# The down projection of a hybrid encoder block: another order of its seven products

## The chip, the cores and the metric

The kernel runs on one NeuronCore of one Trainium2 chip. The metric is the device time of one execution in microseconds (us), lower is better; the times shown are medians over executions on the chip.

## The reference

One layer of an encoder for 512 tokens of width 2048, all in float32. Cut to what matters here:

```python
D_MODEL, SEQ, D_FF = 2048, 512, 5632

def reference(x, g_mix, w_in, ..., w_out, g_ffn, w_gate_up, w_down, g_final):
    h = rmsnorm(x, g_mix[layer])
    proj = jnp.einsum('bsd,de->bse', h, w_in[layer])
    ...                                   # two kinds of attention over the parts of proj
    x = x + jnp.einsum('bse,ed->bsd', mixed, w_out[layer])
    h2 = rmsnorm(x, g_ffn[layer])
    gate, up = jnp.split(jnp.einsum('bsd,df->bsf', h2, w_gate_up[layer]), 2, axis=-1)
    x = x + jnp.einsum('bsf,fd->bsd', jax.nn.silu(gate) * up, w_down[layer])
    return rmsnorm(x, g_final)
```

The change is in the product with `w_down` (5632 x 2048).

## The kernel before, in words

**Products in fp32 from three.** A float32 operand is split into a high and a low half of the reduced type fp32r. `mm3` then issues three matmuls (lines 242, 243, 244): high by high, high by low, low by high.

**Seven products for eight.** The big projections go by 2x2 blocks in a form with seven products, m1 to m7, where a plain one has eight. Each product needs a left operand (a "form" of the activations, computed once, parked in DRAM as `forms`) and a right one of the weights. In the down stage m1, m2 and m3 use a weight tile as it was loaded; m7, m6, m5 and m4 use a sum or difference of two tiles, which VectorE (DVE) computes at line 872 in `weights`.

**Blocks and units of the down stage.** The inner dimension is cut into groups of 6, 8 and 8 pairs of row tiles (`DOWN_PAIRS`), and each group is done for two halves of the columns, so there are six blocks, which the text counts from 0 to 5. In a block each of the seven products has 6 or 8 *units*, one for a pair: a block has 42 or 56 units. A unit is one entry of the list `units`; its product is six matmuls on TensorE (PE), two row tiles by three. Before them stand, for a unit with a sum, the sum on DVE (line 872); then for every unit the high half of the weights on ScalarE (ACT, line 828) and the low half on DVE (line 831). The halves go into one of eight `tw` pairs, so the high half of unit u waits for the matmuls of unit u - 8.

**What sets the order.** One Python loop goes through the units. `prepare` issues the high halves as long as they are planned within `COLS_AHEAD` = 8.0 us of the present unit (a unit counts 1.37) and the low half of all but the last of these; `load_raws` issues the weight loads (tiles `raw`, on SyncE's queue) as far as `COLS_LOAD` = 20.0 us ahead. Then come the unit's matmuls, then what was hooked to its number with `box.after`. Each engine executes its instructions in the order in which they were issued, ACT's DMA issues among its activations.

**Banks.** A product's units accumulate in PSUM. m1, m6, m5 and m3 share the pair of banks called z, m7 and m4 have y, m2 has x. After the last unit of a product ACT evicts the pair (tiles `ev`, line 1216, two instructions) and GpSimd adds it to the result in DRAM. The sums in a shared bank go on: m6 accumulates onto m1 after the eviction of m1, m5 onto m6 after that of m6. So the first unit of m6 and of m5 waits for that eviction.

**Forms of the next group.** Forms that are done with give place to those of the next group. `next_forms` hooks, for each form and each four pairs: a load on ACT's queue into one of two tiles `fr` (line 1190), the high half on ACT (line 1193) and the low half on DVE (line 1196), 128 x 1024 each. They spread from the end of one group into the first block of the next.

**The order of the products** in the blocks but the last, for n pairs, is: all m1, all m7, all m6, two of m2, all m5, the rest of m2, all m4, all m3. The names here: `raw_N` weight tiles, `tw_N` pairs of halves, `arenaN` the forms in place, `fr_N` forms as loaded, `ev_N` evicted rows, `bN` PSUM banks.

Of the kernel before, what the change touches and what calls it, by code (L numbers as in the profile page):

```python
# [64 lines left out]
def f32(ap):  # L65
    return ap.bitcast(F32)
# [3 lines left out]
def encoder_block(ctx, tc, x, g_mix, w_in, g_q_a, g_k_a, g_out_a, g_out_b, w_out, g_ffn,  # L70
# [80 lines left out]
    def form_tile(m, pairs):  # L151
        return arena[0][:, m, pairs] if m < EARLY else arena[1][:, m - EARLY, pairs]
# [99 lines left out]
    def in_turn(tiles, n, shape, dtype, tag):  # L252
        if not tiles and homing[0]:
            whole = sp.tile([P, n] + shape[1:], dtype, tag=tag + "s", bufs=1, name=nm(tag))
            tiles.extend(whole[:, i] for i in range(n))
        if not tiles:
            tiles.extend(sp.tile(shape, dtype, tag=tag, bufs=n, name=nm(tag)) for _ in range(n))
        tiles.append(tiles.pop(0))
        return tiles[-1]

    class Raw:
        def __init__(self, pieces, first=0, tag="raw", width=2 * 512):
            self.pieces, self.first, self.tag, self.width, self.t = pieces, first, tag, width, None
# [46 lines left out]
    def hook(n, f):  # L310
        hooks.setdefault(n, []).append(f)
# [486 lines left out]
    def drain_until(cond):  # L798
        while not cond():
            side.popleft()()  # L800

    CHAIN = ("m1", "m7", "m6", "m2", "m5", "m4", "m3")
# [4 lines left out]
    KEPT = {"m1": (("a",), "a"), "m7": (("c", "b"), "b"), "m6": (("b", "a"), "b"), "m2": (("d",), "d"),  # L807
            "m5": (("c", "b"), "a"), "m4": (("d", "b"), "b"), "m3": (("c",), "c")}


    class Cols(Unit):
# [21 lines left out]
        def mm(self, u):  # L833
            self.box.multiply(self)

    class ColBlock:
        def __init__(self, w, row, lo, pairs, plan, tag, ready=None, close=None, chain=CHAIN, apart=False):
            self.pairs, self.plan, self.ready, self.close = pairs, plan, ready, close
            self.banks = dict(CHAIN_BANK, m3="x") if apart else CHAIN_BANK
            self.last_of_bank = LAST_OF_BANK + ("m5",) if apart else LAST_OF_BANK  # L840
            self.opening = ("m1", "m7", "m2") + (("m3",) if apart else ())
            self.ps, self.at, self.held = {}, {}, []

            def raw(i, j, q):
                at = row + (2 * q + i) * P
                pieces = lo[j] if isinstance(lo[j], list) else [(lo[j], 0, 512)]
                return Raw(lambda t: [(w[0, at:at + P, c:c + n], t[:, dst:dst + n]) for c, dst, n in pieces],
                           tag=tag, width=512)
            kinds = {"a": (0, 0), "b": (0, 1), "c": (1, 1), "d": (1, 0), "e": (0, 1), "f": (1, 0), "g": (1, 1)}
            self.raws = [{n: raw(i, j, q) for n, (i, j) in kinds.items()} for q in range(pairs)]  # L850
            order = [(form, q) for form in chain for q in range(pairs)]
            if ready is not None:
                rest = order[6:8] + order[8:3 * pairs] + order[3 * pairs + 6:]
                order = order[:6] + order[3 * pairs:3 * pairs + 6] + rest
            if plan is KEPT:
                at = 3 * pairs + 2
                behind = 2 if close is not None else 1
                order[at:at + (1 + behind) * pairs - 2] = (order[at + pairs - 2:at + (1 + behind) * pairs - 2]
                                                           + order[at:at + pairs - 2])
            for form, q in order:  # L860
                self.at[form] = len(units)
                src, dst = plan[form]
                need = src + (dst,) if dst not in src else src
                units.append(Cols(self, form, q, [self.raws[q][n] for n in need]))
                if close is not None and form == CHAIN[-1]:
                    units[-1].dur = COLS_US / 2
# [305 lines left out]
    for f in range(0, NFF, 4):  # L1172
        box = gate_up_block(f)
# [4 lines left out]
            nc.gpsimd.dma_start(x1[c, t], x1_dram[c, t])  # L1178

    def next_forms(box, first, pairs):  # L1180
        seq = sorted(CHAIN, key=box.at.get)

        def ready(form, h):
            m, st = ORDER.index(form), {}
            lo_q, n = 4 * h, min(4, pairs - 4 * h)
            hi, lo = (form_tile(m, slice(lo_q, lo_q + n))[:, :, j] for j in range(2))

            def load():
                st["t"] = in_turn(frs, 2, [P, 4, 256], F32, "fr")[:, :n]
                nc.scalar.dma_start(st["t"], forms_dram[:, m, first + lo_q:first + lo_q + n])  # L1190

            def split_hi():
                nc.scalar.activation(hi, st["t"], AF.Copy)

            def split_lo():
                nc.vector.tensor_tensor(lo, st["t"], f32(hi), op=OP.subtract)  # L1196
            late = 4 * seq.index(form) + 4 * h
            box.after(form, late - 5, load)
            box.after(form, late + 1, split_hi)
            box.after(form, late + 3, split_lo)  # L1200
        for form in seq:
            for h in range(-(-pairs // 4)):
                ready(form, h)
# [121 lines left out]
    for n in DOWN_PAIRS:  # L1325
        next_forms(box, first, n)
        for cb in range(2):
            box = down_block(first, n, cb, (first + n, cb) == (NFF // 2, 1))
        first += n

    at = [0.0]
# [142 lines left out]
```

## Time and profile before

| | |
|---|---|
| time, median of 3 runs | 1985.04 us (1984.05 to 1986.88) |
| the profiled execution | 1985.48 us, of which the span of the trace is 1983.7 us |
| PE busy | 1968.0 us, 99% of the span |
| DVE busy | 1589.3 us, 80% |
| ACT busy | 1131.0 us, 57% |
| mean granted clock of PE | 0.998 |

The down stage runs from about 1549 us to 1970 us of the span. Busy times of PE are modelled from pipelined matmuls, so a PE that is always busy still shows where it loses time: by the distance between the starts of its matmuls, and by the granted clock (1.00 is full speed).

### The profile page before, as it was taken

Reading aid. Unit: us, or ns where it says so; the run is one execution under the profiler, and the core shown is the slowest. Engines: PE = TensorE matmul, PEld = TensorE weight load, DVE = VectorE, ACT = ScalarE, POOL = GpSimd, SP = SyncE. Lnnn points to the kernel's source line nnn. Section 1 sums busy time; section 2 is a strip of 40 time slices with the busy share of each in tenths; the row PEclk is TensorE's granted clock in tenths of the full one; section 3 lists DMA queues with packets and bytes.
Section 4 is the critical chain, followed back from the end, with each engine's and each line's share of the span. In section 5 each row is a group of like instructions: output and inputs, shape, how many; then the busy total and the mean of one; then the engine's idle time right before and its main releaser. Section 6 shows DMA issues by size and latency. Waiting matters only on the chain.

```text
span 1983.7 us, 27526 instructions
## 1 busy us (share of the span) xinstructions
PE 1968.0 (99%) x8972; PEld 1623.0 (82%) x8972; DVE 1589.3 (80%) x2725; ACT 1131.0 (57%) x2071; POOL 120.4 (6%) x162
## 2 busy tenths in 40 slices
PE   9999999999999999999999999999999999999998
PEld 7888887888888888888888888888888888788886
DVE  6888678888775698887878878878879987887977
ACT  7655555565555565555555555545556666666655
POOL 0100001000000000000000000000000121111121
PEclk9999999999999999999999999999999999999999
DMA  8576683143343564755836737657458699769765
GB/s 278 181 281 206 214 276 125 66 144 128 117 151 105 196 206 164 278 167 188 298 124 242 258 128 267 216 174 278 159 192 285 189 276 251 196 158 268 198 162 173
DMA packets 235873, 394.83 MB, mean 199 GB/s; under 512 B 22560, under 2 KB 77648, under 8 KB 235600
## 3 DMA queue, kind: packets, MB, share of 16 engines
q1 hardware_dynamic: 211440, 330.85, 49.6%
q0 software_dynamic: 17200, 40.38, 9.3%
q10 hardware_dynamic: 7088, 21.83, 3.2%
q8 instruction: 70, 1.15, 0.2%
q14 instruction: 75, 0.61, 0.1%
HBM read 330.33 MB, written 62.65 MB: 198 GB/s over the span
## 4 chain that ended last, share of the span: by engine, by line
PE 94%; DVE 3%; ACT 1%; DMA 1%; issue 1%; ACTq 0%; POOL 0%; POOLq 0%; DVEq 0%; SPq 0%
PE b L242 30%; PE b L244 30%; PE b L243 30%; PE b L600 1%; PE b L1145 1%; DMA raw<-in_w_in_dram 1%; DVE raw L872 0%; DVE tw L831 0%; PE b L1069 0%; PE b L326 0%; PE b L550 0%; DVE arena L1196 0%; DVE w L300 0%; ACT rj L435 0%; DVE ra L448 0%
## 5 line engine op out<-in xcount | busy, mean ns | idle before, releaser
L242 PE MATMUL b<-tw,arena 128*128 128x512 f32 x2244 | 880.0, 392 | 2.2 <-ACT ev L1216 2.2
L243 PE MATMUL b<-tw,arena 128*128 128x512 f32 x2244 | 874.6, 390 | 0.3 <-DVE tw L300 0.3
L244 PE MATMUL b<-tw,arena 128*128 128x512 f32 x2244 | 874.6, 390 | 0.0
L828 ACT ACTIVATE tw<-raw 128x512 fp32r<-128x512 f32 x924 | 558.3, 628 | 434.3 <-DVE raw L872 271.6
L831 DVE TENSOR_TENSOR tw<-raw,tw 128x512 fp32r<-128x512 f32 x924 | 618.8, 687 | 167.6 <-ACT tw L828 164.6
L242 PEld LDWEIGHTS b<-tw,arena 128*128 128x128 f32 x2244 | 421.8, 188 | 88.6 <-ACT ev L1216 2.9
L243 PEld LDWEIGHTS b<-tw,arena 128*128 128x128 f32 x2244 | 422.0, 188 | 88.1 <-DVE tw L831 1.4
L244 PEld LDWEIGHTS b<-tw,arena 128*128 128x128 f32 x2244 | 421.7, 188 | 88.2
L872 DVE TENSOR_TENSOR raw<-raw,raw 128x512 f32<-128x512 f32 x528 | 361.1, 685 | 1.4 <-DMA raw<-in_w_gate_up_dram 1.4
L1217 POOL DMA_DIRECT2D x1d<-ev x76 | 66.4, 981 | 1149.3 <-ACT ev L1216 1144.2
L828 ACT ACTIVATE tw<-stage 128x512 fp32r<-128x512 f32 x140 | 85.4, 629 | 67.7 <-DVE stage L872 46.5
L831 DVE TENSOR_TENSOR tw<-stage,tw 128x512 fp32r<-128x512 f32 x140 | 93.6, 687 | 23.5 <-ACT tw L828 23.4
L242 PE MATMUL b<-w,arena 128*128 128x512 f32 x240 | 95.8, 399 | 0.0
L233 ACT ACTIVATE pTh<-b 128x512 fp32r<-128x512 f32 x64 | 38.3, 598 | 100.3 <-PE b L600 96.4
L244 PE MATMUL b<-w,arena 128*128 128x512 f32 x240 | 93.9, 391 | 0.0
L243 PE MATMUL b<-w,arena 128*128 128x512 f32 x240 | 93.5, 390 | 0.0
L365 DVE TENSOR_TENSOR pair<-pair 128x256 f32<-128x256 f32 x120 | 45.5, 421 | 25.0 <-ACT pair L1072 23.9
L1216 ACT ACTIVATE ev<-b,smalls 128x512 f32<-128x512 f32 x76 | 49.6, 682 | 26.3 <-PE b L244 25.3
L1120 DVE TENSOR_TENSOR s<-b,s 128x512 f32<-128x512 f32 x66 | 44.0, 688 | 24.7 <-PE b L244 24.7
L244 PEld LDWEIGHTS b<-w,arena 128*128 128x128 f32 x240 | 45.0, 188 | 10.0
L243 PEld LDWEIGHTS b<-w,arena 128*128 128x128 f32 x240 | 45.2, 188 | 9.1
L242 PEld LDWEIGHTS b<-w,arena 128*128 128x128 f32 x240 | 45.1, 188 | 8.8
(210 smaller groups left out, 1778.9 us busy)
## 6 DMA issues: line engine op xcount, KB each, us to landing
raw<-in_w_gate_up_dram SPq DMA_DIRECT2D x616, 256.0 KB, 5.3
raw<-in_w_down_dram SPq DMA_DIRECT2D x176, 256.0 KB, 6.9
stage<-in_w_in_dram SPq DMA_DIRECT2D x111, 256.0 KB, 5.0
forms<-pair SPq DMA_DIRECT2D x22, 896.0 KB, 5.3
x1d<-ev POOLq DMA_DIRECT2D x76, 256.0 KB, 6.5
fr<-forms ACTq DMA_DIRECT2D x35, 512.0 KB, 6.0
raw<-in_w_out_dram SPq DMA_DIRECT2D x32, 512.0 KB, 4.9
stage<-in_w_in_dram SPq DMA_DIRECT2D x90, 128.0 KB, 3.5
```

Of the source, the lines that this page charges most:

```text
L233: nc.scalar.activation(hi, src, AF.Copy)
L242: nc.tensor.matmul(dst, ah, bh, start=start, stop=False, skip_group_check=chained)
L243: nc.tensor.matmul(dst, ah, bl, start=False, stop=False, skip_group_check=chained)
L244: nc.tensor.matmul(dst, al, bh, start=False, stop=stop, skip_group_check=chained)
L365: nc.vector.tensor_tensor(out, x, y, op=op)
L600: nc.tensor.transpose(ps[:, t * P:(t + 1) * P], self.p[t][:, kb * P:(kb + 1) * P], ident)
L828: nc.scalar.activation(self.pair[:, 0], self.src, AF.Copy)
L831: nc.vector.tensor_tensor(self.pair[:, 1], self.src, f32(self.pair[:, 0]), op=OP.subtract)
L872: nc.vector.tensor_tensor(t[dst], t[src[0]], t[src[1]], op=OP.add if form == "m6" else OP.subtract)
L1120: nc.vector.tensor_tensor(d[:, t], box.bank_of(form)[t], d[:, t], op=OP.add)
L1216: nc.scalar.activation(e, box.bank_of(form)[t], AF.Copy, scale=r2["r"][:, row:row + 1])
L1217: nc.gpsimd.dma_start(x1_dram[2 * cb + j, row], e, accum_op=OP.add)
```

## The change

It puts the units of the down stage's blocks 0 to 4 into another order (block 5, the last, keeps its own). After three units of m1, units of m7 and m1 alternate until both are used up; m6, two of m2 and m5 follow as before; then the rest of m2 alternates with all but the last four of m4, and those four alternate with the first of m3. So in a block of eight pairs m1 ends with unit 12 where it ended with unit 7, and m7 with unit 15 as before; in a block of six pairs m1 ends with unit 8 where it ended with unit 5, and m7 with unit 11. `next_forms` takes the new ends of the products, and puts at least four units between two forms; a load still stands six units before its high half.

```diff
+    def kept_order(pairs):
+        def mixed(a, b, lead):
+            a, b, out = deque(a), deque(b), []
+            for _ in range(lead):
+                out.append(a.popleft())
+            while a or b:
+                if b:
+                    out.append(b.popleft())
+                if a:
+                    out.append(a.popleft())
+            return out
+
+        def some(form, lo, hi):
+            return [(form, q) for q in range(lo, hi)]
+        n = pairs
+        return (mixed(some("m1", 0, n), some("m7", 0, n), 3) + some("m6", 0, n) + some("m2", 0, 2) + some("m5", 0, n) + mixed(some("m2", 2, n), some("m4", 0, n - 4), 1)
+                + mixed(some("m4", n - 4, n), some("m3", 0, n), 1))
...
-            if plan is KEPT:
+            if plan is KEPT and close is None:
+                order = kept_order(pairs)
+            elif plan is KEPT:
                 at = 3 * pairs + 2
-                behind = 2 if close is not None else 1
-                order[at:at + (1 + behind) * pairs - 2] = (order[at + pairs - 2:at + (1 + behind) * pairs - 2]
-                                                           + order[at:at + pairs - 2])
+                order[at:at + 3 * pairs - 2] = (order[at + pairs - 2:at + 3 * pairs - 2]
+                                                + order[at:at + pairs - 2])
...
-        seq = sorted(CHAIN, key=box.at.get)
+        seq, turns = sorted(CHAIN, key=box.at.get), [0]
...
-            late = 4 * seq.index(form) + 4 * h
-            box.after(form, late - 5, load)
-            box.after(form, late + 1, split_hi)
-            box.after(form, late + 3, split_lo)
+            turn = max(box.at[form] + 4 * seq.index(form) + 4 * h + 1, turns[-1] + 4)
+            turns.append(turn)
+            hook(turn - 6, load)
+            hook(turn, split_hi)
+            hook(turn + 2, split_lo)
```

The new lines move the numbers of those behind them: the sum is line 891 in the new kernel, the form's load, high half and low half are 1209, 1212 and 1215, the eviction is 1236; lines 828 and 831 stay.

On DVE, the opening of block 2 before, from the low half of unit 2 (`tw_549`) on:

```order
L831 TENSOR_TENSOR tw_549_5951<-raw_1277_13989,tw_549_5951 128x512
L1196 TENSOR_TENSOR arena5_86<-fr_1174_12534,arena5_86 128x4x256
L831 TENSOR_TENSOR tw_550_5952<-raw_1278_14001,tw_550_5952 128x512
L831 TENSOR_TENSOR tw_543_5945<-raw_1279_14011,tw_543_5945 128x512
L831 TENSOR_TENSOR tw_544_5946<-raw_1280_14023,tw_544_5946 128x512
L831 TENSOR_TENSOR tw_545_5947<-raw_1281_14033,tw_545_5947 128x512
L1196 TENSOR_TENSOR arena5_86<-fr_1175_12535,arena5_86 128x4x256
L872 TENSOR_TENSOR raw_1284_14059<-raw_1283_14057,raw_1284_14059 128x512
L831 TENSOR_TENSOR tw_546_5948<-raw_1282_14043,tw_546_5948 128x512
```

And after, from the low half of unit 1 (`tw_548`) on:

```order
L831 TENSOR_TENSOR tw_548_5950<-raw_1276_13973,tw_548_5950 128x512
L891 TENSOR_TENSOR raw_1279_13997<-raw_1278_13995,raw_1279_13997 128x512
L831 TENSOR_TENSOR tw_549_5951<-raw_1277_13984,tw_549_5951 128x512
L1215 TENSOR_TENSOR arena5_86<-fr_1174_12534,arena5_86 128x4x256
L831 TENSOR_TENSOR tw_550_5952<-raw_1279_13997,tw_550_5952 128x512
L891 TENSOR_TENSOR raw_1282_14026<-raw_1281_14024,raw_1282_14026 128x512
L831 TENSOR_TENSOR tw_543_5945<-raw_1280_14012,tw_543_5945 128x512
L831 TENSOR_TENSOR tw_544_5946<-raw_1282_14026,tw_544_5946 128x512
L891 TENSOR_TENSOR raw_1285_14049<-raw_1284_14047,raw_1285_14049 128x512
L831 TENSOR_TENSOR tw_545_5947<-raw_1283_14037,tw_545_5947 128x512
L1215 TENSOR_TENSOR arena5_86<-fr_1175_12535,arena5_86 128x4x256
```

The first sum of m7 (the first row that reads and writes `raw` tiles) stood behind the low half of unit 6 and a form's low half; now it stands ahead of the low half of unit 2, and low halves of units without a sum come between the sums.

On ACT, further on in block 2, up to the eviction of m6 that m5's first unit waits for (`ev_1242`, `ev_1243`); `tw_549`, `tw_550` and `tw_543` are units 26 to 28, the first three of m5. Before:

```order
L828 ACTIVATE tw_548_5950<-raw_1300_14255 128x512
L828 ACTIVATE tw_549_5951<-raw_1275_13962 128x512
L828 ACTIVATE tw_550_5952<-raw_1276_13974 128x512
L1190 DMA fr_1175_12535<-forms_135 128x1024
L828 ACTIVATE tw_543_5945<-raw_1277_13989 128x512
L1216 ACTIVATE ev_1242_13252<-b3_74,smalls_82 128x512
L1216 ACTIVATE ev_1243_13253<-b1_72,smalls_82 128x512
```

And after:

```order
L828 ACTIVATE tw_548_5950<-raw_1300_14249 128x512
L828 ACTIVATE tw_549_5951<-raw_1275_13962 128x512
L1212 ACTIVATE arena5_86<-fr_1175_12535 128x4x256
L828 ACTIVATE tw_550_5952<-raw_1276_13973 128x512
L828 ACTIVATE tw_543_5945<-raw_1277_13984 128x512
L1209 DMA fr_1175_12535<-forms_135 128x1024
L1236 ACTIVATE ev_1242_13286<-b3_74,smalls_82 128x512
L1236 ACTIVATE ev_1243_13287<-b1_72,smalls_82 128x512
```

The load of a form (`fr_1175`) stood ahead of the high half of unit 28; it now stands behind it, directly ahead of the eviction.

## The prediction

> **What bounds the kernel now.** I began with the page's head and with a table of stretches, one for each block of the down stage (the stage that the change touches), and went from there to the only stretch in which TensorE loses time.
>
> ```profile
> span 1983.7 us, 27526 instructions
> 1549.00:1608.00 59.00, 58.44 (x266) 48.18 (x265) 51.00 (x84) 36.28 (x62) 10.57 (x12) 1.00 0.77 199
> 1666.00:1746.00 80.00, 78.24 (x334) 63.44 (x334) 64.74 (x98) 48.13 (x79) 12.18 (x14) 0.98 0.77 204
> 1746.00:1822.00 76.00, 76.00 (x337) 62.94 (x336) 61.68 (x94) 48.08 (x78) 12.21 (x14) 1.00 0.78 200
> 1822.00:1898.00 76.00, 76.00 (x337) 62.96 (x336) 62.98 (x97) 47.26 (x77) 12.23 (x14) 1.00 0.81 219
> PE b L242 <- ACT ev L1216: 2.2, 2, 1.7
> ```
>
> The columns of the stretches are: length, then busy time (count) of PE, PEld, DVE, ACT and POOL, the granted clock, the DMA share and GB/s. TensorE (PE) is busy for 76.00 of 76.00 us in blocks 3 and 4. Only block 0 (58.44 of 59.00) and block 2 (78.24 of 80.00, clock 0.98) lose anything, and in the whole stage PE waits twice, for evictions. So a new order can gain only what those two blocks lose. The timeline of PE in block 2 shows what that is.
>
> ```profile
> 1686.24 0.39 PE L242 MATMUL b<-tw,arena 128*128 128x512 f32 x1
> 1686.61 0.50 PE L243 MATMUL b<-tw,arena 128*128 128x512 f32 x1
> 1686.95 0.40 PE L244 MATMUL b<-tw,arena 128*128 128x512 f32 x1
> ...
> 1700.36 0.39 PE L242 MATMUL b<-tw,arena 128*128 128x512 f32 x1
> 1700.83 0.50 PE L243 MATMUL b<-tw,arena 128*128 128x512 f32 x1
> 1701.16 0.40 PE L244 MATMUL b<-tw,arena 128*128 128x512 f32 x1
> ...
> 1701.87 0.39 PE L244 MATMUL b<-tw,arena 128*128 128x512 f32 x1
> 1703.93 0.79 PE L242 MATMUL b<-tw,arena 128*128 128x512 f32 x1 [1.68 <-ACT ev L1216]
> ...
> 1707.46 0.39 PE L244 MATMUL b<-tw,arena 128*128 128x512 f32 x1
> ...
> 1709.07 0.39 PE L242 MATMUL b<-tw,arena 128*128 128x512 f32 x1
> ...
> 1710.43 0.39 PE L242 MATMUL b<-tw,arena 128*128 128x512 f32 x1
> 1700.00:1705.00 5.00, 3.24 (x12) 2.02 (x11) 4.99 (x9) 3.59 (x7) 0.71 (x2) 0.90 0.49 145
> 1705.00:1710.00 5.00, 5.00 (x19) 4.03 (x18) 4.82 (x7) 2.60 (x4) 1.03 (x2) 0.76 0.95 209
> ```
>
> From 1709.07 to 1710.43 six matmuls start, which is one unit: 1.36 us (a pitch of 0.227). Against that pitch, the step from 1701.87 to 1703.93 loses 1.83 us: product m5[0], unit 26, waits for ScalarE (ACT) to evict m6 from its bank. From 1703.93 to 1707.46 eight pitches take 3.53 instead of 1.82, 1.71 us more: the granted clock has fallen (0.90 and 0.76 in the two stretches). Two short delays of late low halves stand before it: 1686.24 to 1686.95 is 0.71 for two pitches (0.25 lost) and 1700.36 to 1701.16 is 0.80 (0.35 lost). Block 2 thus loses 1.83 + 1.71 + 0.60 = 4.14 us.
>
> **Why the eviction is late.** VectorE (DVE) and ACT around it:
>
> ```profile
> 1671.85 1.22 DVE L1196 TENSOR_TENSOR arena<-fr,arena 128x1024 fp32r<-128x1024 f32 x1
> 1672.98 0.68 DVE L872 TENSOR_TENSOR raw<-raw,raw 128x512 f32<-128x512 f32 x1
> 1673.59 0.69 DVE L831 TENSOR_TENSOR tw<-raw,tw 128x512 fp32r<-128x512 f32 x1
> ...
> 1701.90 0.68 DVE L872 TENSOR_TENSOR raw<-raw,raw 128x512 f32<-128x512 f32 x1
> 1662.30 1.16 ACT L828 ACTIVATE tw<-raw 128x512 fp32r<-128x512 f32 x2 [3.22 <-DMA raw<-in_w_down_dram]
> 1667.31 0.63 ACT L828 ACTIVATE tw<-raw 128x512 fp32r<-128x512 f32 x1 [1.86 <-DVE arena L1196]
> ...
> 1702.68 0.63 ACT L828 ACTIVATE tw<-raw 128x512 fp32r<-128x512 f32 x1 [0.57 <-DVE raw L872]
> 1703.21 1.25 ACT L1216 ACTIVATE ev<-b,smalls 128x512 f32<-128x512 f32 x2
> ```
>
> ACT works in order, and the eviction (1703.21) stands behind the high split of unit 28 (1702.68), which waits for that unit's weight sum on DVE (1701.90). DVE is late because the sums begin only at 1672.98, after the m1 units that need none. Before that ACT was held up at the block's opening (3.22 and 1.86 us) and DVE starved behind it. From then on sixteen units in a row (m7, m6) need a sum and a low split. One such step is 1672.98 to 1673.59, 0.61 us, so a unit takes 1.21 us of DVE, and a form's low half takes 1671.85 to 1672.98, 1.13 us, about every four units. That makes 1.21 + 0.28 = 1.49 us for a unit, against 1.36 on PE: a deficit of 0.13 us a unit that eats the lead.
>
> **The change, part by part.** The instructions stay the same in number; only their places differ. (1) *m1 and m7 alternate*: in 24 units DVE has 8 sums among the first 16 units, spread from unit 3 on, in place of 8 in a row from unit 8. An alternating pair takes 3 steps and half a form, 1.83 + 0.57 = 2.40 us, of the 2.72 that PE takes: the lead grows by 0.16 us a unit instead of shrinking. The sums of m7 fill the time in which DVE starved in m1. (2) *m1's bank*: m1 now ends at unit 12 and not at 7, and m6, at unit 16, accumulates in the same bank, so its eviction has 3 units to spare, 4.08 us, where it had 8. An eviction's price and the other terms:
>
> ```profile
> 1680.26 1.25 ACT L1216 ACTIVATE ev<-b,smalls 128x512 f32<-128x512 f32 x2
> 1680.92 0.33 ACTq L1190 DMA_DIRECT2D fr<-forms  x1
> 1681.40 0.63 ACT L828 ACTIVATE tw<-raw 128x512 fp32r<-128x512 f32 x1
> ...
> 1695.61 0.63 ACT L828 ACTIVATE tw<-raw 128x512 fp32r<-128x512 f32 x1 [0.57 <-DVE raw L872]
> 1696.28 0.69 DVE L831 TENSOR_TENSOR tw<-raw,tw 128x512 fp32r<-128x512 f32 x1 [0.16 <-ACT tw L828]
> L1216 ACT ACTIVATE ev<-b,smalls 128x512 f32<-128x512 f32 x76 | 49.6, 682 | 26.3 <-PE b L244 25.3
> L1190 ACTq EVENT_SEMAPHORE  x27: 17/17/3471, 1527.1 to 1849.8; - x27
> ```
>
> Two evictions take 1.14 us from 1680.26 to 1681.40, one alone 0.68 (mean of the group). So the new wait of m6[0] ends 13 x 1.361 + 0.68 = 18.4 us into the block, against a need at 16 x 1.361 = 21.8: 3.4 us of cover, and in a block of six pairs the same three units. I cost it at nothing; without that cover it would cost its lateness, at most the 1.83 of the row above. (3) *The wait of m5[0] for m6's eviction* stays. I work out its lateness by a ledger from the end of m1's pair of evictions at 17.7 + 1.14 = 18.85 us: a high split to the low split behind it 0.67 (1695.61 to 1696.28); seven sums and ten low splits for units 18 to 28, 17 x 0.60 = 10.2; two form halves 2.3; and about 0.75 in which DVE waits while ACT evicts m7 (my estimate: two thirds of a pair's 1.14); together 32.8. There the form's load (line 1209 in the new kernel) now stands directly ahead of the eviction on ACT's queue, where one high split stood between them. It costs 0.45 by 1680.92 to 1681.40, so 33.2; the first eviction ends at 33.9. The need is 26 x 1.361 = 35.4, so 1.5 us are spare. Blocks 1, 3 and 4 come out at 1.3 to 2.0 by the same sum. That load's price is the uncertain term: it can't be below nothing, and its upper bound is the longest that such an issue has stood waiting, 3.47 us in the last row (min/median/max of the issue's wait in ns). I take 0.45 because at least half of those 27 waits took 17 ns. (4) *m2/m4 and m4/m3 alternate*: m4's sums spread over units that need none, and nothing waits there now (blocks 3 and 4 lose nothing), so nothing is gained. (5) *Raw loads* on SP's queue keep their look-ahead, and the alternating units need 1.5 tiles each instead of one and then two. (6) *Form loads* keep six units, 8.2 us, between issue and use.
>
> ```profile
> 1577.51 0.60 PE L1145 MATMUL b<-fixed,s 128*128 128x128 f32 x4
> 1578.67 0.50 PE L242 MATMUL b<-tw,arena 128*128 128x512 f32 x1 [0.56 <-ACT ev L1216]
> DMA to landing us min/median/max: 2.6/6.8/11.7
> DMA to landing us min/median/max: 3.4/6.0/8.7
> ```
>
> The landings are the raw tiles' (first row) and the forms' (second). Raw tiles are asked for 20 us ahead and split 8 us ahead, 12 us against at most 11.7; both prices are nothing, with up to 0.5 us (8.7 less 8.2) at the worst form. In block 0 PE waits 0.56 us at 1578.67. The eviction it waits for stands behind the transposes of line 1145 as well, which stay, so removing the late sums frees between nothing and all of it; I count half, 0.28.
>
> **The sum.** 4.14 + 0.28 = 4.42 us less. The profiled execution took 1985.48 us, its span 1983.7; the median of the three runs shown, 1985.04, is 0.44 below it. 1985.48 - 4.42 - 0.44 = 1980.6.
>
> The fall of the clock weighs 1.71 of it. Here it follows a gap of 1.83 us, and after the 0.56 gap of block 0 the clock stayed at 1.00, so I hold the gap to be the cause. The Trainium skill ("TensorE: Matmul & The Clock Gate", Why this matters for your kernels) asks for gaps under about 3 us and lets the clock fall after an idle window of 3.4; the trace does not agree, since it falls after 1.83, and the measurement decides.
>
> **The rivals.**
> - *One or two stalls remain or are new.* ACT is still held at a block's opening (3.22 and 1.86 above) and the ledger's spare 1.5 us is used up in one or two blocks. A stall like the old one costs 1.83 + 1.71 = 3.5: 1980.6 + 3.5 = 1984.1, or 1987.6 with two. For it speaks that the ledger's spare is smaller than one long issue; against it that blocks 3 and 4 pass today with 0.13 us a unit of deficit. 26%.
> - *Slower: the form's load blocks m6's eviction in most blocks.* The load waits, in ACT's order, for DVE to have read the same buffer and for a free queue slot; a form's low half that comes 1.5 us later than the ledger has it decides. Each block then loses 3.5: three of five give 1980.6 + 10.5 = 1991.1, all five 1998.1. For it speaks the 3.47 us issue, and that high split which no longer stands between; against it the DVE lead that now grows in m1/m7. 17%.
> - *The spell at half clock has a cause of its own and stays.* Then 4.42 - 1.71 = 2.71 are gained: 1985.04 - 2.71 = 1982.3. 4%.
> - *The more frequent turning between banks brings spells of half clock*, one in each changed block: 5 x 1.71 = 8.55, so 1989.2. Against it stands clock 1.00 in blocks 3 and 4, whose units each already turn between two banks. 3%. The Trainium skill (same page, A second HAM failure mode: psum-queue depth-cycling) describes a clock that swings because a kernel cycles through PSUM banks; no row here shows that.
>
> **How the numbers follow.** 0.2%, about what a measurement of this kernel can tell from no change, is 3.97 us: faster is below 1981.07, slower above 1989.0. The forecast has 50%, at 1980.6; it lies 0.5 under the bound, so I count 40% as faster and 10% as same. Same adds the 26% and the 4%, slower is 17% + 3%. The range starts 1.0 below the forecast, as the lowest run lies below its median, and 0.3 more for the rest of block 0's wait: 1979.3. It ends at two stalls, 1987.6, which leaves out the 20% of slower.
>
> **What would show it.** Right: no wait of PE for an eviction in block 2 at unit 26, its stretch about 76 us long and at clock 1.00, the sums of m7 on DVE starting about when its first product does and not 7 us later, and evictions of m1 ending 3 us before m6[0]. Wrong: in blocks 0 to 4 waits of line 242 for line 1236 (the eviction's line in the new kernel), with a form load waiting just ahead on ACT, or a block below clock 1.00 without a gap.

## The result, and the profile after

The changed kernel takes 1982.02 us (median of 17 runs, 1979.99 to 1983.23), the kernel before, in as many runs beside it, 1986.35 (1984.01 to 1988.06). The ratio is 0.9979, with a 95% interval of 0.9972 to 0.9985: 4.3 us less, where 4.4 were forecast. The size was right; the experiments show that the reason was not.

The profiled execution of the changed kernel took 1982.76 us, with a span of 1981.0. These are the stretches of its blocks 0, 2, 3 and 5 (columns as in the prediction; its block 2 starts at 1666.81), and PE's waits in the whole down stage:

```profile
1549.00:1608.00 59.00, 59.00 (x269) 48.65 (x268) 50.57 (x83) 37.53 (x64) 10.58 (x12) 1.00 0.74 197
1666.00:1744.00 78.00, 78.00 (x346) 64.59 (x345) 65.64 (x99) 49.12 (x81) 12.57 (x15) 1.00 0.85 214
1744.00:1820.00 76.00, 76.00 (x337) 62.94 (x336) 63.49 (x96) 48.25 (x78) 11.79 (x14) 1.00 0.84 216
1896.00:1968.00 72.00, 71.69 (x315) 58.70 (x314) 65.28 (x110) 43.99 (x91) 19.21 (x30) 1.00 0.57 147
PE b L243 <- DVE tw L831: 0.2, 1, 0.2
```

Blocks 0 and 2 lose nothing now, no matmul waits for an eviction, and the clock stays at 1.00. Block 5, full before (72.00 of 72.00), has lost 0.31 us; no run was spent on that. The next lines are from ACT, DVE and PE around block 2:

```profile
1658.53 0.33 ACTq L1209 DMA_DIRECT2D fr<-forms  x1
1658.96 0.63 ACT L828 ACTIVATE tw<-raw 128x512 fp32r<-128x512 f32 x1
...
1684.37 0.67 ACT L1236 ACTIVATE ev<-b,smalls 128x512 f32<-128x512 f32 x1
...
1700.51 0.33 ACTq L1209 DMA_DIRECT2D fr<-forms  x1
1700.94 0.69 ACT L1236 ACTIVATE ev<-b,smalls 128x512 f32<-128x512 f32 x1 [1.52 <-DVE arena L1215]
1666.81 0.39 PE L242 MATMUL b<-tw,arena 128*128 128x512 f32 x1
...
1702.17 0.39 PE L242 MATMUL b<-tw,arena 128*128 128x512 f32 x1
1672.12 0.69 DVE L831 TENSOR_TENSOR tw<-raw,tw 128x512 fp32r<-128x512 f32 x1
```

Three things are to be seen. First, the load of a form at 1658.53, just ahead of block 2's first high half (1658.96), goes out while ACT is still at work: ACT doesn't stand. In the trace of before the same load went out at 1661.93 and the high half behind it came after 3.22 us of idle time, put down to a weight tile's landing (the prediction shows that row). Second, m6's eviction at 1700.94 comes after ACT has stood for 1.52 us behind a form's load; it ends at 1701.63, and m5's first matmul, the 157th of the block, starts at 1702.17: only 0.5 us were to spare. Third, the low half of unit 7 ends at 1672.81. Its product is due seven units after 1666.81, at 1676.33, so DVE leads by 3.5 us. The same sum before, from the block's first matmul at 1665.84 and a low half ending at 1674.28, gives 1.1.

I call this the lead at unit 7; it is used below. So DVE is not ahead because block 2's order lets it gain: it enters the block ahead.

### The profile page after: what moved, and what is told of

The parts are those of the page before. It is cut to its first block, busy times and chain, and to the rows that moved or that the text cites. A ratio compares the mean times of both kernels' runs of the same rounds, so it can differ in the third digit from the quotient of the medians.

```text
span 1981.0 us, 27522 instructions
## 1 busy us (share of the span) xinstructions
PE 1968.1 (99%) x8972; PEld 1623.2 (82%) x8972; DVE 1591.4 (80%) x2725; ACT 1130.1 (57%) x2071; POOL 120.4 (6%) x162
## 4 chain that ended last, share of the span: by engine, by line
PE 94%; DVE 2%; issue 2%; DMA 1%; ACT 1%; POOL 0%; SPq 0%; POOLq 0%; DVEq 0%; ACTq 0%
PE b L242 30%; PE b L244 30%; PE b L243 30%; PE b L600 1%; PE b L1164 1%; DMA x<-x1d 0%; PE b L1088 0%; DMA x1d<-ev 0%; PE b L550 0%; PE b L326 0%; DVE w L300 0%; ACT rj L435 0%; DMA stage<-in_w_in_dram 0%; DMA raw<-in_w_in_dram 0%; DVE ra L448 0%
## 5 line engine op out<-in xcount | busy, mean ns | idle before, releaser
L828 ACT ACTIVATE tw<-raw 128x512 fp32r<-128x512 f32 x924 | 556.4, 628 | 425.3 <-DVE raw L891 289.0
L244 PEld LDWEIGHTS b<-w,arena 128*128 128x128 f32 x240 | 45.0, 188 | 10.0
L1167 ACT ACTIVATE pair<-b 128x512 f32<-128x512 f32 x44 | 26.3, 597 | 47.0 <-PE b L1164 46.7
L243 PEld LDWEIGHTS b<-w,arena 128*128 128x128 f32 x240 | 45.2, 188 | 9.1
```

The costliest lines, as they stand in the source:

```text
L243: nc.tensor.matmul(dst, ah, bl, start=False, stop=False, skip_group_check=chained)
L244: nc.tensor.matmul(dst, al, bh, start=False, stop=stop, skip_group_check=chained)
L828: nc.scalar.activation(self.pair[:, 0], self.src, AF.Copy)
L1167: nc.scalar.activation(st["pair"][:, half * 1024:half * 1024 + 512], ps, AF.Copy)
```

## The experiments

Theory 1 is the prediction's: m7's sums in a row, behind units without sums, use up DVE's lead inside block 2. Theory 2 is that block 1's alternating tail and the places of the form loads free ACT where block 2 opens. After the first four runs it became theory 3: what matters is whether ACT stands at a form's load at the end of block 1. Theory 4: what matters is where in block 2 the forms' low halves lie. All times are compared with the kernel before on the same chip (medians 1985.7 to 1986.0 in these runs). "m1, m7, ..." in a diff stands for `some("m1", 0, n)` and so on; the diffs are shortened, and `block`, `old_order`, `later[form]` and `held` in them stand for longer code.

**Half of the new order.** The alternating head alone, then the alternating tail alone:

```diff
-mixed(m1, m7, 3) + m6 + m2[0:2] + m5 + mixed(m2[2:], m4[:n-4], 1) + mixed(m4[n-4:], m3, 1)
+mixed(m1, m7, 3) + m6 + m2[0:2] + m5 + m2[2:] + m4 + m3                       # e1
+m1 + m7 + m6 + m2[0:2] + m5 + mixed(m2[2:], m4[:n-4], 1) + mixed(m4[n-4:], m3, 1)   # e2
```

> Only m1 and m7 alternate (blocks 0 to 4); m2, m4 and m3 stand in a row as before. Theory 1 (m7's sums begin too late and in a row, so the lead of DVE is gone by m6's eviction): the whole gain, 4.0 to 4.6 us less than before, no wait of PE at m5[0] of block 2, the block at clock 1.00. Theory 2 (the alternating tail of block 1 and the shifted form loads free ACT at block 2's opening): the wait of 1.3 to 1.8 us and the half clock stay, within 0.5 us of before.

> Only m2/m4 and m4/m3 alternate (blocks 0 to 4); all m1 stand before all m7 as before. Theory 1: PE's wait at m5[0] of block 2 and the half clock behind it stay, 0 to 1 us less than before. Theory 2: the wait is gone, 4.0 to 4.6 us less.

The head alone: 1984.81 us, ratio 0.9994 (0.9986 to 1.0003). The tail alone: 1983.16, 0.999 (0.9981 to 0.9999). The first line below is ACT with the head alone, the others are PE's wait at m5[0] of block 2, head alone and tail alone:

```profile
1662.95 1.15 ACT L828 ACTIVATE tw<-raw 128x512 fp32r<-128x512 f32 x2 [4.41 <-DMA raw<-in_w_down_dram]
1702.91 0.50 PE L242 MATMUL b<-tw,arena 128*128 128x512 f32 x1 [1.59 <-ACT ev L1235]
1702.07 0.50 PE L242 MATMUL b<-tw,arena 128*128 128x512 f32 x1 [1.12 <-ACT ev L1236]
```

Theory 1 had the whole gain from the head; the wait stayed at 1.59 us, and PE waited 0.47 us at a new place, m6[0] of block 2. The tail took the wait at m5[0] down only to 1.12 and gained 2.7 us, so neither expectation held fully, and the two halves act together.

**The new order in some blocks only.** `kept_order` in block 2 alone, and in all but block 2:

```diff
-                order = kept_order(pairs)
+                order = kept_order(pairs) if block == 2 else old_order(pairs)     # e7; e8: block != 2
```

> The new order in block 2 alone, the old one in blocks 0, 1, 3, 4. Theory 1: block 2 loses nothing, the wait of 0.5 us in block 0 stays: 3.5 to 4.2 us less than before. Theory 2: block 2's opening is set by block 1's tail, which is old here, so the wait stays: within 1 us of before.

> The new order in blocks 0, 1, 3, 4, the old one in block 2. Theory 1: block 2 loses about 4 us as before and only block 0's 0.3 to 0.7 us is gained. Theory 2: the wait in block 2 is gone, 4.0 to 4.6 us less than before.

In block 2 alone: 1983.91 us, 0.9988 (0.9979 to 0.9996), and PE waits 1.42 us at m5[0]. The gain of 1.9 us lies between the two theories' ranges: the wait is only 0.26 shorter than before's, but the spell at half clock is not in this trace. In all but block 2: 1982.15 us, 0.9983 (0.9974 to 0.9992), and PE waits for no eviction. Block 2 is cured by the order of the other blocks. Block 1 is the one just ahead:

```diff
+                order = kept_order(pairs) if block == 1 else old_order(pairs)     # e13; e14: block != 1
```

> The new order in block 1 alone. Theory 3: block 1's alternating tail takes the hold away, the lead at block 2's first unit is 4.5 us or more, the wait at m5[0] of block 2 is 0 to 1.3 us, nothing else is lost there: 2 to 4 us less than before. Theory 1: block 2 has its sums in a row as before, the wait stays at 1.8 us or so.

> The new order in blocks 0, 2, 3 and 4, the old one in block 1. Theory 3: ACT is held 3 us or more at the end of block 1, the lead at block 2's first unit is 2.5 us or less and the wait at m5[0] 1.2 to 1.9 us: at most 2.5 us less than before. Theory 1: as fast as the changed kernel, 4 us less.

In block 1 alone: 1982.67 us, 0.998 (0.9971 to 0.9989), as fast as the whole change within the intervals. In all but block 1: 1982.01 us, 0.9984 (0.9975 to 0.9993). Blocks 0 and 2 and the end of block 1 on ACT for e13, then ACT and PE for e14:

```profile
1549.00:1609.00 60.00, 59.44 (x270) 49.00 (x269) 52.24 (x85) 36.23 (x62) 10.59 (x12) 1.00 0.75 196
1666.00:1744.00 78.00, 78.00 (x346) 64.59 (x345) 64.30 (x98) 49.65 (x80) 13.60 (x16) 1.00 0.83 219
1658.64 0.35 ACTq L1211 DMA_DIRECT2D fr<-forms  x1
1658.68 2.70 ACT L828 ACTIVATE tw<-raw 128x512 fp32r<-128x512 f32 x5
```

```profile
1660.32 0.33 ACTq L1211 DMA_DIRECT2D fr<-forms  x1
1660.69 1.15 ACT L828 ACTIVATE tw<-raw 128x512 fp32r<-128x512 f32 x2 [3.12 <-DMA raw<-in_w_down_dram]
...
1701.28 0.50 PE L242 MATMUL b<-tw,arena 128*128 128x512 f32 x1 [1.43 <-ACT ev L1238]
```

With the new order in block 1 alone, block 2 is full (78.00 of 78.00) though its own order is the old one, and ACT goes through the form's load without a stop; block 0's wait is left, 59.44 of 60.00. Without block 1, ACT stands for 3.12 us again and PE for 1.43. In the traces that decides against theory 1 as the account of the wait.

The times do not decide it: e14 gained 3.7 us, about what theory 1 had, where theory 3 allowed at most 2.5. The program ahead of the stage is the same in all kernels, but the time it takes is not: block 0's first matmul starts at 1549.52 us in the trace of before, at 1550.51 in the changed kernel's and at 1548.03 in e14's. From there to PE's last matmul they take 425.3, 421.6 and 422.6 us, so in its one trace e14's stage is 1.0 us longer than the changed kernel's. Of the 2.7 us that it gains on before's, 1.71 is the spell at half clock, which e14's trace does not have.

**The load, or its place.** Three kernels with the order of before in all blocks. In e11 the forms come at the units of the new order; in e12 one load, the held one, goes two units earlier; in e9 the loads of the later groups leave from GpSimd's queue, and e10 is the same with the new order.

```diff
-            turn = max(box.at[form] + 4 * seq.index(form) + 4 * h + 1, turns[-1] + 4)
+            turn = max(box.at[form] + later[form] + 4 * seq.index(form) + 4 * h + 1, turns[-1] + 4)   # e11
-            hook(turn - 6, load)
+            hook(turn - (8 if held else 6), load)                                              # e12
-                nc.scalar.dma_start(st["t"], forms_dram[...])
+                (nc.gpsimd if box.plan is KEPT else nc.scalar).dma_start(st["t"], forms_dram[...])   # e9, e10
```

> The order of before in all blocks, but the forms of the next group are loaded and split at the units at which the new order does it (m1 3 or 5, m2 2 or 4, m4 3 units later). Theory 3: the load at the boundary keeps its unit and still waits for the same weight tile, ACT is held about 3 us, the wait at m5[0] stays at 1 us or more, less than 1.5 us gained. Theory 4 (the places of the forms' low halves on DVE in block 2 decide): the wait is gone, 3 to 4.5 us less than before.

> The order of before in all blocks; one single form load (the second half of m5's form, asked for at the end of block 1) is issued two units earlier, so that by the order its issue waits for the 17th weight tile of block 2 where it waited for the 20th. Theory 3 (the 3.2 us for which ACT stands still there cost block 2 its lead): ACT isn't held more than 1 us, the lead at block 2's first unit is 4.5 us or more (2.2 before), the wait at m5[0] is under 0.6 us: 2.5 to 4.5 us less than before. Theory 4 (the order of the sums and the places of the forms' low halves inside block 2 decide): the wait stays above 1.2 us, less than 1.5 us gained.

> The order of before in all blocks; the form loads of the second and third group are issued on GpSimd's queue where they were on ACT's, and nothing else. Theory 3 (what costs the lead in before is that ACT stands still for 3.2 us at the boundary of blocks 1 and 2, held by a form load's issue that waits for a weight tile to land): ACT isn't held there, the lead at block 2's first unit is 4.5 us or more where it was 2.2, and the wait of 1.8 us at m5[0] is gone or under 0.5 us: 3 to 4.5 us less than before. Theory 1 (the sums of m7 in a row behind m1's units): the wait stays at 1.3 us or more, at most 1.5 us gained.

> The new order, with the form loads of the second and third group on GpSimd's queue. Theory 3: no wait of PE at m5[0] in any block and about the time of the changed kernel (within 0.7 us); ACT is no longer held 1.66 us ahead of m6's eviction in block 2, so that the eviction ends 1.5 to 2 us ahead of its need where it ended 0.5 ahead. Theory 1: the same time, and the eviction no earlier, since its place in the order is what counts.

Measured: e11 1985.83 us, 1.0001 (0.9992 to 1.001); e12 1982.93, 0.9985 (0.9976 to 0.9994); e9 1988.79, 1.0014 (1.0005 to 1.0023); e10 1982.01, 0.9981 (0.9972 to 0.9989). ACT where block 2 opens and PE's wait at m5[0], first in e11 (with the stretch of the wait, clock 0.79), then in e12; then ACT in e9, and last e10, where the third row is PE's wait at m5[0] of block 4:

```profile
1664.25 1.15 ACT L828 ACTIVATE tw<-raw 128x512 fp32r<-128x512 f32 x2 [3.71 <-DMA raw<-in_w_down_dram]
1705.58 0.55 PE L242 MATMUL b<-tw,arena 128*128 128x512 f32 x1 [2.50 <-ACT ev L1236]
1703.00:1708.00 5.00, 2.50 (x7) 1.95 (x7) 4.49 (x8) 3.49 (x7) 1.75 (x2) 0.79 0.80 235
```

```profile
1660.36 0.63 ACT L828 ACTIVATE tw<-raw 128x512 fp32r<-128x512 f32 x1 [2.65 <-DMA raw<-in_w_down_dram]
1704.04 0.50 PE L242 MATMUL b<-tw,arena 128*128 128x512 f32 x1 [1.26 <-ACT ev L1235]
```

```profile
1664.17 1.06 ACT L1211 ACTIVATE arena<-fr 128x1024 fp32r<-128x1024 f32 x1 [3.58 <-DMA fr<-forms]
1671.18 1.06 ACT L1211 ACTIVATE arena<-fr 128x1024 fp32r<-128x1024 f32 x1 [2.71 <-DMA fr<-forms]
```

```profile
1664.02 1.06 ACT L1212 ACTIVATE arena<-fr 128x1024 fp32r<-128x1024 f32 x1 [2.41 <-DMA fr<-forms]
1700.48 0.50 PE L242 MATMUL b<-tw,arena 128*128 128x512 f32 x1 [0.17 <-ACT ev L1236]
1854.21 0.50 PE L242 MATMUL b<-tw,arena 128*128 128x512 f32 x1 [1.08 <-ACT ev L1236]
```

e11 has the forms where the new order has them, and still the hold (3.71, and 2.17 more for a form's landing) and a wait of 2.50: their places alone do not help, and theory 4 falls as a sole cause. In e12 one load moved by two units gains 2.8 us, which speaks for theory 3, though the hold only shrank to 2.65 where I expected under 1, the lead at the first unit is 3.3 where I expected 4.5, and PE still waits 1.26. e9 went against its expectation, 2.8 us slower with a wait of 1.68, and does not test theory 3: ACT no longer stands at the issue but, 3.58 and 2.71 us, for the form itself. With the same queue the new order (e10) is 6.8 us faster than the old (e9) and takes the changed kernel's time, as expected, but it has waits at m5[0] where none was expected: 0.17 us in block 2, where the eviction was to end early, and 1.08 in block 4.

The lead at unit 7 of block 2, worked out as above from each trace, beside the longest time for which ACT stands where block 2 opens for a transfer (a load's issue or a form's landing; waits for PE and DVE left out) and PE's wait at m5[0] of block 2:

| kernel | block 1's order | ACT stands, us | lead at unit 7, us | PE waits, us |
|---|---|---|---|---|
| before | old | 3.22 | 1.1 | 1.68 |
| e9, GpSimd's queue | old | 3.58 | 0.0 | 1.68 |
| e1, head only | old tail | 4.41 | 0.1 | 1.59 |
| e11, new places of forms | old | 3.71 | 0.4 | 2.50 |
| e7, block 2 only | old | 3.33 | 1.3 | 1.42 |
| e14, not block 1 | old | 3.12 | 1.3 | 1.43 |
| e12, one load earlier | old | 2.65 | 2.4 | 1.26 |
| e2, tail only | old head | 1.83 | 2.1 | 1.12 |
| e8, not block 2 | new | 0.41 | 3.5 | none |
| e13, block 1 only | new | none | 3.6 | none |
| changed kernel | new | none | 3.5 | none |
| e10, GpSimd's queue | new | 2.41 | 1.0 | 0.17 |

In these twelve, with 3.5 us of lead there is no wait, whatever the order inside block 2; with 2.4 or less there is one. But the length of the wait does not follow the lead: e10 has no more of it than before and ACT stands 2.41 us, yet PE waits only 0.17. In e10 no form's load stands on ACT ahead of m6's eviction, where the changed kernel spends 1.52 us; so the lead is not the whole account.

**Two doses of cover.** In the new order, m2's two units between m6 and m5 moved behind m5 in block 2 (e4); one unit of m1 ahead of the alternation in place of three, in all five blocks (e6):

```diff
-... + m6 + m2[0:2] + m5 + mixed(m2[2:], ...)
+... + m6 + m5 + mixed(m2, ...)               # e4, block 2
-mixed(m1, m7, 3) + ...
+mixed(m1, m7, 1) + ...                       # e6
```

> The new order, but in block 2 no unit of m2 stands between m6 and m5 (two did). The changed kernel's trace has m6's first eviction ending 0.5 us ahead of m5's first matmul there, so taking 2.72 us away should make PE wait 2.2 us at m5[0]; by the prediction's ledger (1.5 us spare) it would be 1.2 us. If a gap of 1.8 us is enough to lower the clock, 3.4 us at half clock follow; if it depends on something else, a gap of 2.2 us can pass at full clock.

> The new order with one unit of m1 ahead of the alternation where three stood: m1 ends with unit 14 (10 in the blocks of six) and its eviction has one unit, 1.36 us, until m6's first product in the same bank, where it had three. By the changed kernel's trace the first eviction ended 3.5 us ahead of that need in block 2; 2.72 less leaves 0.8 if ACT is free, and m7's evictions there were about 0.8 us late behind a sum: waits of PE at m6[0] of 0 to 1 us in each of five blocks, 0 to 4 us more than the changed kernel, none at half clock.

e4 was run once, 1986.21 us; e6 took 1985.76, 1.0001 (0.9992 to 1.0009), which gives all of the gain back. PE's waits and the stretches behind them, first e4, then e6:

```profile
1702.19 0.80 PE L242 MATMUL b<-tw,arena 128*128 128x512 f32 x1 [3.03 <-ACT ev L1239]
1698.00:1703.00 5.00, 1.97 (x8) 1.34 (x7) 4.74 (x7) 3.16 (x6) 0.46 (x1) 0.89 0.80 220
1703.00:1708.00 5.00, 5.00 (x18) 3.98 (x18) 4.63 (x7) 3.01 (x6) 1.30 (x2) 0.77 0.90 207
```

```profile
1691.65 0.50 PE L242 MATMUL b<-tw,arena 128*128 128x512 f32 x1 [1.76 <-ACT ev L1236]
1690.00:1695.00 5.00, 3.35 (x15) 2.78 (x16) 4.60 (x8) 4.61 (x9) 2.64 (x3) 1.00 0.48 117
1695.00:1700.00 5.00, 5.00 (x24) 4.14 (x23) 4.90 (x8) 3.00 (x5) 0.85 (x1) 1.00 1.06 166
```

Without m2's units there PE waits 3.03 us, more than the 2.2 worked out, since the sums of m5 come earlier too and the eviction stands behind two more of them. In e6 the wait is a new one, at m6[0], for m1's eviction: 1.76 us in block 2 alone, where I had put up to 1 us in each block. In block 2 the three units that the change leaves there are needed.

## Why the prediction was right, and where it was not

- **The time and the terms.** Forecast 1980.6 us and 4.4 less; measured 1982.02 and 4.3 less. The loss of block 2 went as a whole, as the sum had it. It did not go for the reason given, so that the number agrees is in part luck.
- **The step that failed** is the reason under "Why the eviction is late", and part (1) built on it: that sixteen units with sums in a row, from 1672.98 on, use up the lead, so that alternating m1 and m7 in block 2 mends it. The new order in block 2 alone left a wait of 1.42 us (e7), in block 1 alone it left none (e13). I had both rows of ACT's hold (3.22 and 1.86) before me, named them as what came first, and then priced only the part after it.
- **Part (4)** cost the alternating tail at nothing, because nothing waits in the tail. It is a part of what brings the gain: a form's load that is issued beside the tail of block 1 no longer finds ACT standing. In the program, that load's issue waits, in ACT's order, for the landing of an earlier transfer of SP's queue: the 20th weight tile of block 2 in the old order, the 18th in the new one; by the semaphores in the traces the issue follows that landing by about 0.1 us. The Trainium skill ("DMA: Bandwidth & Descriptors", Anatomy of one DMA — SWDGE (gpsimd) path) states that a wait on a semaphore is served by the issuing engine's sequencer before dispatch; the 3.22, 3.12 and 4.41 us in which ACT does nothing agree, for loads on ACT's queue. The place in the order is not all: e12's load follows the 17th tile and ACT still stands 2.65 us, as that tile takes 9.0 us from issue to landing; before's 20th takes 10.6, the changed kernel's 18th 5.6.
- **Part (3), the ledger**, gave 1.5 us to spare at m5[0]; it was 0.5. The mis-sized term is the form's load directly ahead of the eviction: 0.45 taken, 1.52 measured, inside the bound of 3.47. So the rival of a load that blocks the eviction came within 0.5 us of deciding block 2.
- **Part (2)** had 3.4 us of cover for m6[0]. The first eviction of m1 ended at 1685.04, 3.5 us ahead of m6's first matmul (16 units after 1666.81, 1688.57).
- **Block 0**: half of 0.56 us was counted; the stretch is full now, so all of it went, from the block's own alternating head: e1, with the head alone, has no wait there, and e2 and e13 without it keep 0.56 (59.44 of 60.00).
- **The clock.** 1.71 us of the sum stood on the gap of 1.68 us as cause. The size holds: the spell is 3.41 us at clock 0.50 (the first row below), and half of that is 1.71. The gap's length is not the whole cause. Gaps of 1.12 to 1.76 us (e2, e12, e7, e14, e1, e6) passed at clock 1.00, and so did one of 1.68 in e9 (the second row, and the stretch from that gap on in the third); those of 2.50 and 3.03 (e11, e4) did not.

```profile
1703.97:1707.38 3.41, 3.41 (x8) 2.74 (x9) 3.22 (x6) 3.00 (x5) 1.75 (x2) 0.50 0.92 264
1705.52 0.49 PE L242 MATMUL b<-tw,arena 128*128 128x512 f32 x1 [1.68 <-ACT ev L1235]
1704.49:1707.91 3.42, 2.39 (x10) 1.99 (x11) 3.36 (x6) 3.42 (x6) 1.79 (x2) 1.00 0.66 216
```

In all three traces with such a spell it begins a whole number of steps of 3.413 us after full clock was first granted: 498 in before (1703.97 less 4.14), 496 in e4 (1701.93 less 8.92), 497 in e11 (1705.89 less 9.47). So where a gap falls against these steps may decide; that is not shown. Before's spell need not be in all of its runs, and how much of the measured 4.3 us is clock stays open: of the other runs only the mean clock is on record, and e7's profiled run reads 0.998, as before's does, without such a spell.

- **Open** too is whether the hold by itself carries the whole effect. In the traces block 1's order decides the wait, but it moves two things together: the hold, and the places of the forms' loads in block 2. In e13, for one, a load stands directly ahead of m6's eviction (1700.57 and 1700.99), as in the changed kernel, though block 2 has its old order. e11 moved the places and kept the hold, e12 shortened the hold and kept the places; no run has the old places and no hold.

## What to carry to other kernels

When an engine's lead runs out, look for where it was lost, not for where it is missed: here the order of block 1, at whose end ACT stood 3 us at a transfer's issue, decided whether PE waited for an eviction 40 us later. Before a reordering is credited to the block where the time comes back, put it into one block at a time. A transfer issued from a compute engine's own queue can hold that engine for an unrelated transfer, so its place beside the other queues' transfers is part of the schedule.

## What the runs showed of the hardware

Gaps of PE between 1.1 and 1.8 us were followed by a spell at half clock in one trace (before, 1.68 us) and in none of e1, e2, e6, e7, e9, e12 and e14 (1.59, 1.12, 1.76, 1.42, 1.68, 1.26, 1.43); the longer ones, 2.50 and 3.03 us, were in both cases. Each of the three spells lasted 3.41 us at clock 0.50. A form's load on ACT's queue kept ACT standing for up to 4.41 us, until another queue's transfer had landed (e1). The same 512-KB form loads, moved to GpSimd's queue, made ACT wait up to 3.58 us for their landing, and the kernel with before's order was 0.14% slower.
